# A two-block network on one core: memory laid out transposed, a split per-layer product, and an inverse that is transposed

## The chip, the cores and the metric

The kernel runs on one core of one Trainium2 chip. Its time is that of one execution on the device, in microseconds (us); three runs give a median. A profile of one further execution shows every instruction of each engine: TensorE (PE) with its weight loads (PEld), VectorE (DVE), ScalarE (ACT), GpSimd (POOL), and SyncE (SP), which issues nearly all DMAs.

## The reference

All of it is float32. There are 256 tokens of width 1024, which pass through two blocks of two layers each; everything is needed to float32 precision.

```python
def first_block(x, p, ...):                    # layers 0 and 1
    h = x
    for layer in range(2):
        hn = rmsnorm(h, gains[0])
        mix = mixer_ab(hn, ...) if layer == 0 else mixer_c(hn, ...)
        h = h + rmsnorm(mix, gains[1])
        ff = square(relu(rmsnorm(h, gains[2]) @ w_up)) @ w_down      # 1024 x 4096 x 1024
        h = h + rmsnorm(ff, gains[3])
        gate = sigmoid(h @ w_ple_gate)                               # 1024 x 1024
        h = h + gate * (p[layer] @ w_ple)                            # p: 256 x 256, w_ple: 256 x 1024
    return h

def gated_delta_rule(...):                     # in mixer_ab: 4 heads, chunks of 64 tokens
    lmat = where(strict, (kb @ k.T) * decay, 0)
    uw = triangular_solve(lmat + eye, rhs)     # the inverse of a unit lower triangular matrix
    ...

def second_block(x, mem, ...):                 # two layers more
    for l in range(2):
        xn = rms_norm(x, attn_norm[l])
        # five groups of heads on xn @ w_in[l]; the fifth attends to the memory:
        mem_kv = rms_norm(mem, mem_norm[l]) @ mem_w_kv[l]            # mem: 256 x 1024, 1024 x 512
        x = x + concat(o_a, o_b, o_c, o_d, o_e) @ w_o[l]
        xn = rms_norm(x, ffn_norm[l])
        x = x + (silu(conv(xn @ ffn_w_gate)) * (xn @ ffn_w_up)) @ ffn_w_down
```

## The kernel before

**Products.** A float32 value is split in two parts of a type for which PE needs one pass (fp32r): `hi`, the rounded copy, and `lo`, the rest. A product is then three matmuls, hi x hi, lo x hi and hi x lo. Plain float32 operands go through PE in two passes. `block` (L770) fetches 1 MB of weights into one of two tiles `raw` (512 KB and less for some), and splits it in four parts: a copy to one of four tiles `hi` (ACT, or DVE where that is free) and a subtraction to one of four tiles `lo` (DVE). `whole` (L783) loads a block straight into a `hi` tile and leaves it in plain float32. `aTh` and `aTl` hold the two parts of the transposed activations. `stream` runs a list of blocks through three matmuls for each product; `nmm` issues those of one slice, `tmm` those whose result comes out transposed.

**Stages, with the stretch of the profiled execution.** The first mixer with the delta rule (10 to 202 us; its weights are w0g, w0t, w0n and w0o), the first feed-forward (211 to 394, wu and wd), the gate of layer 0 (398 to 422, wg), the second mixer (424 to 512, w1n and w1o), the second feed-forward (522 to 704) and its gate (707 to 731), then the second block: mixers of layer 0 (731 to 891, wk, wi, wm, wo), its gated feed-forward (897 to 1088, fg, fu, fd), the mixers of layer 1 (1088 to 1234) and its feed-forward (to 1425).

**The order.** The code doesn't issue instructions as it runs: a recorder collects every operation (so nearly all rows of the profile carry its line, L610), and a list scheduler then sets the order of the whole program on every engine, operation by operation, from a table of prices (`price`), of delays between engines (`LAG`), and of the tiles that each pool has. Coroutines (`loom`) yield where work of other parts may be put between. `per_layer_input` is thus only a place in the recorded program: its matmuls are used as filler wherever the planner sees PE free and their operands ready. The borders between stages, where the residual, a norm and the transposes of the next input run, have little other work.

**What the change touches.** The inverse in the delta rule (a loop over six levels, for two pairs of heads, each with 4 matrices of 128x128 side by side): a level has a product `mb` with X, a copy, and two products `yb` and `xb` that give the next Y and the next X, which is Y's transpose. `per_layer_input` (called for layer 0 ahead of the first feed-forward and for layer 1 ahead of the second mixer) computes p @ w_ple in plain float32. `memory_T` and `memory` load the memory (four DMAs for each of the two layers of the second block), multiply it with a gain that is spread over all partitions (a DMA of 512 KB), find its root mean square, transpose it on PE, and run wk's product.

Of the kernel before, what the change touches and what calls it, by code (L numbers as in the profile page):

```python
# [50 lines left out]
for _l in range(2):  # L51
    for _n in ("mla_q", "mla_k", "fox_q", "fox_k", "moba_q", "moba_k", "diff_q", "diff_k", "mem_q", "mem_k"):
        _put(COLS, f"{_n}{_l}", 1)
    _put(COLS, f"fconv{_l}", 22 * 4)
NCOLS = sum(w for _, w in COLS.values())

# [81 lines left out]
def layout(x):  # L138
    f32 = np.float32
    A = {}  # L140
    A["x"] = x["x"].reshape(2, P, D)
    A["memx"] = x["mem_2"].reshape(2, P, D)
    pp = x["p"].reshape(2, 256, 2, P)
    A["pT"] = pp.transpose(0, 3, 2, 1).reshape(2, P, 512)
# [58 lines left out]
    for l in range(2):  # L203
        setc(f"mla_q{l}", np.concatenate([one[:32], x["mla_q_norm_2"][l][32:]]))
        setc(f"mla_k{l}", np.concatenate([one[:32], x["mla_k_norm_2"][l][32:]]))
        for s in ("q", "k"):
            setc(f"fox_{s}{l}", np.concatenate([x[f"fox_{s}_norm_2"][l], one[:1]]))
            m = np.concatenate([one[:16], x[f"moba_{s}_norm_2"][l][16:]])
            setc(f"moba_{s}{l}", np.tile(m, 2))
            d = np.concatenate([one[:8], x[f"diff_{s}_norm_2"][l][8:]])  # L210
            setc(f"diff_{s}{l}", np.tile(d, 4))
            setc(f"mem_{s}{l}", np.tile(x[f"mem_{s}_norm_2"][l], 2))
        cw = np.concatenate([x["ffn_conv_w_2"][l], x["ffn_conv_b_2"][l][None]], 0)
        setc(f"fconv{l}", cw.reshape(4, 22, P).transpose(2, 1, 0).reshape(P, 88))
# [40 lines left out]
class Recorder:  # L255
# [9 lines left out]
           "pool": {"pe": 200, "act": 90, "dve": 69, "pool": 97, "sp": 1220},  # L265
           "sp": dict.fromkeys(("pe", "act", "dve", "pool", "sp"), 910)}

# [121 lines left out]
    def price(self, op, out, ins):  # L389
# [18 lines left out]
        if op.eng == "pool":  # L408
# [4 lines left out]
            return 235 + 5 * n if op.call == "tensor_tensor" else 260 + 4 * n + 190 * per_row  # L413
        return 50 + P * n * (2 if out.dtype == BF16 else 4) / 366.0

# [242 lines left out]
def program(ctx, tc, A, out, dbg=None):  # L658
# [33 lines left out]
    def f(ap):  # L692
        return ap.bitcast(F32)
# [42 lines left out]
    aTl = cpool.tile([P, 8, 256], F32R, name="aTl")  # L736
    cpool.tile([P, 16], F32, name="behind")

# [31 lines left out]
    def block(name, i, k, w):  # L770
# [10 lines left out]
        return fold(hi[:, :n], k), fold(lo[:, :n], k)  # L781

    def whole(name, i, k, w):  # L783

        t = rec.new("hi", NHL, hlp.tile([P, 2048], F32R, tag="hi", name=nm("hi")))
        n = k * w
        sp.dma_start(out=f(t[:, :n]), in_=A[name][i])
        return fold(f(t[:, :n]), k)

# [302 lines left out]
    def mixer_ab(end):  # L1092
# [109 lines left out]
        def delta(hp):  # L1202
# [39 lines left out]
            for lv in range(1, 7):  # L1242
# [10 lines left out]
                for i in range(4):  # L1253
                    pe.matmul(yb[:, i, :], m[:, i, :], Y[:, i, :], start=True, stop=True)
                if lv < 6:
                    xb = wk(4)
                    for i in range(4):
                        pe.matmul(xb[:, i, :], Y[:, i, :], m[:, i, :], start=True, stop=True)
                    xn = w2(4)
                    dve.tensor_tensor(xn, X, xb, op=OP.subtract)  # L1260
                    X = xn
                yn = w2(4)
                dve.tensor_tensor(yn, Y, yb, op=OP.subtract)
                Y = yn
            yield
            hs = slice(2 * hp, 2 * hp + 2)
# [227 lines left out]
    def per_layer_input(l):  # L1494

        pr, pw = w2(2), {}
        sp.dma_start(out=flat(pr), in_=A["pT"][l])
        w = whole(f"wp{l}", 0, 2, 1024)
        for t in range(2):
            pw[t] = [w2(), w2()]  # L1500
            for q in range(2):
                b = acc()
                for k in range(2):
                    pe.matmul(b, pr[:, k, ts(t)], halves(w[:, k, :])[q], start=(k == 0), stop=(k == 1))
                rec.copy(pw[t][q], b, 0.5)
        return pw
# [102 lines left out]
    def heads_T(t, x, dst, k, g):  # L1609

        b = transposes([x(i) for i in range(4)])
        for i in range(2):
            rec.copy(dst[i][:k, :, ts(t)], b[:k, 2 * i : 2 * i + 2, :], col(g)[:k])

    def memory_T(l):

        g = gain(12 + l)
        parts, r = {}, {}

        def chain(t):  # L1620
            xm, xs = [w2(), w2()], [w2(), w2()]
            for q in range(2):
                sp.dma_start(out=xm[q], in_=A["memx"][t][:, q * 512 : (q + 1) * 512])
                dve.tensor_tensor(xs[q], xm[q], halves(g)[q], op=OP.mult)
            r[t], _ = rms(xm)
            yield
            for q in range(2):
                parts[t, q] = four_T(xs[q])
                yield

        for t in range(2):
            loom.spawn(chain(t), ("memT", l, t))
        return parts, r

    def memory(l, parts, r):

        kT, v = w2(2), {}

        def prep(t, bank):
            x = w2()  # L1640
            rec.copy(x, bank, r[t])
            kn = w2(8)[:, 0:4, :]
# [8 lines left out]

        loom.join(("memT", l, 0), ("memT", l, 1))
        stream(f"wk{l}", [(0, 0, 0), (0, 1, 4)], lambda t, k: parts[t, k // 4](k % 4), 4, 1, 512, tail_lagged(2, 2), done)
        return kT, v
# [416 lines left out]

    pw = per_layer_input(1)
    mixer_c(rc, out1)
# [11 lines left out]

    ff1(1, e, pw, into2)
    mem = memory(0, *memory_T(0))
    tab, lam = rope_tables2(0)
# [3 lines left out]
    for l in range(2):  # L2092
# [30 lines left out]
        if l == 0:  # L2123
            mem = memory(1, *memory_T(1))
        ff2(l, after)
# [22 lines left out]
```

## Time and profile before

| | |
|---|---|
| median of three runs | 1430.82 us (1430.28 to 1437.37) |
| profiled execution | 1430.91 us, span 1429.1 us |
| PE, PEld busy | 1383.2 us (97%), 1208.5 us (85%) |
| DVE, ACT, POOL busy | 991.2 us (69%), 765.7 us (54%), 119.6 us (8%) |
| mean granted clock of PE | 0.993 of full speed |
| DMA | 236.33 MB, 165 GB/s, 45% of the 16 engines' span |

The span is the stretch from the first to the last instruction that the profiler saw; the time of the execution has 1.8 us around it. A row of stretches gives the width, and for each engine its busy time and in brackets its instructions; PEclk is the granted clock of TensorE as a part of the full 2.4 GHz (0.5 is the lower level, 1.2 GHz). In a row such as `ps<-hi,w 128*128 128x512`, the target stands ahead of the arrow, then the moving operand, then the stationary one; ps is PSUM, w a working tile in SBUF, cf the constants (with the identity for transposes). Two passes of a plain float32 matmul count as two instructions.

### The profile page before, as it was taken

The page shows a single profiled execution, that of the slowest core. Times are in us where ns is not written, and L with a number is a line of the kernel's source. Part 1 is how long each engine was busy: PE and PEld are TensorE (multiplying, and loading weights), DVE is VectorE, ACT ScalarE, POOL GpSimd, SP SyncE. Part 2 cuts the span into 40 slices and gives each one's busy share as a digit, 9 for nine tenths or more (in the row PEclk, how much of TensorE's full clock was granted, in tenths as well). Part 3 has the DMA queues.
Part 4 walks back from the last instruction along what each step waited for, and adds up shares of the span by engine and source line. Part 5 has one row for each costly group of instructions (what it writes and reads, how often), then busy time and mean ns, then how long its engine had stood idle before and what let it go on. Part 6 is the DMA issues. An engine that isn't in the chain of part 4 may idle for free.

```text
span 1429.1 us, 23022 instructions
## 1 busy us (share of the span) xinstructions
PE 1383.2 (97%) x8824; PEld 1208.5 (85%) x8830; DVE 991.2 (69%) x2196; ACT 765.7 (54%) x1760; POOL 119.6 (8%) x140
## 2 busy tenths in 40 slices
PE   6999999999999979999999899999999999999998
PEld 6889879898877669999887777999998777799997
DVE  5995685655677865666768786665757877566664
ACT  5534564443554844444656596554545778464443
POOL 0000120000010010000024301000001511000000
PEclk9999999999999989999999999999999999999999
DMA  8412354545525353455555433345534532345443
GB/s 335 149 60 94 129 191 150 205 180 199 210 103 213 122 189 148 177 187 225 205 172 177 151 130 118 119 177 204 210 147 160 202 140 89 119 152 202 177 179 116
DMA packets 36109, 236.33 MB, mean 165 GB/s; under 512 B 4128, under 2 KB 4384, under 8 KB 9888
## 3 DMA queue, kind: packets, MB, share of 16 engines
q1 hardware_dynamic: 36000, 234.87, 45.4%
q8 instruction: 69, 1.13, 0.3%
q14 instruction: 40, 0.33, 0.1%
HBM read 233.81 MB, written 1.05 MB: 164 GB/s over the span
## 4 chain that ended last, share of the span: by engine, by line
PE 77%; DVE 12%; DMA 4%; ACT 3%; POOL 2%; issue 1%; POOLq 0%; SPq 0%; ACTq 0%; DVEq 0%
PE ps L610 77%; DVE w L610 5%; DVE lo L610 4%; POOL s L610 2%; DVE s L610 2%; ACT w L610 2%; DMA raw<-in_wu 2%; DMA raw<-in_w0t 1%; ACT hi L610 1%; DVE h L610 1%; DMA raw<-in_wg 1%; DMA raw<-in_w1n 0%; DMA raw<-in_wd 0%; ACT L610 0%; DVE aTl L610 0%
## 5 line engine op out<-in xcount | busy, mean ns | idle before, releaser
L610 ACT ACTIVATE hi<-raw 128x512 fp32r<-128x512 f32 (+2 forms) x767 | 424.3, 622 | 381.2 <-PE ps L610 281.9
L610 DVE TENSOR_TENSOR lo<-raw,hi 128x512 fp32r<-128x512 f32 x836 | 520.9, 678 | 66.4 <-ACT hi L610 63.0
L610 PE MATMUL ps<-hi,w 128*128 128x512 f32 (+1 forms) x1272 | 385.5, 401 | 0.3 <-ACT w L610 0.3
L610 PE MATMUL ps<-aTh,hi 128*128 128x256 f32 x1256 | 321.2, 281 | 2.1 <-ACT hi L610 2.1
L610 PE MATMUL ps<-aTl,hi 128*128 128x256 f32 x1256 | 321.8, 280 | 0.2 <-DVE aTl L610 0.2
L610 PE MATMUL ps<-aTh,lo 128*128 128x256 f32 x1256 | 317.5, 281 | 0.0
L610 PEld LDWEIGHTS ps<-hi,w 128*128 128x128 f32 x1272 | 222.0, 188 | 36.7 <-issue 3.8
L610 PEld LDWEIGHTS ps<-aTh,hi 128*128 128x128 f32 x1256 | 226.0, 188 | 13.5 <-ACT hi L610 3.3
L610 PEld LDWEIGHTS ps<-aTl,hi 128*128 128x128 f32 x1256 | 226.6, 188 | 9.4 <-issue 0.9
L610 PEld LDWEIGHTS ps<-aTh,lo 128*128 128x128 f32 x1256 | 224.7, 188 | 10.4 <-issue 0.7
L610 PE MATMUL ps<-lo,w 128*128 128x512 f32 (+1 forms) x620 | 200.0, 393 | 0.0
L610 ACT ACTIVATE w<-ps 128x512 f32<-128x512 f32 (+5 forms) x259 | 125.1, 532 | 132.2 <-PE ps L610 127.1
L610 DVE CAST hi<-raw 128x512 fp32r<-128x512 f32 x69 | 29.4, 426 | 239.2 <-PE ps L610 237.4
L610 PE MATMUL ps<-hi,aTh 128*128 128x512 f32 (+2 forms) x480 | 149.5, 373 | 4.3 <-ACT w L610 3.0
L610 PE MATMUL ps<-lo,aTh 128*128 128x512 f32 (+2 forms) x480 | 147.0, 369 | 2.5 <-DVE lo L610 2.5
L610 PE MATMUL ps<-hi,aTl 128*128 128x512 f32 (+2 forms) x480 | 146.6, 368 | 0.0
L610 POOL TENSOR_TENSOR s<-s,nhalf 128x1 f32<-128x1 f32 (+6 forms) x64 | 80.7, 1269 | 584.9 <-DVE s L610 582.4
L610 PEld LDWEIGHTS ps<-lo,w 128*128 128x128 f32 x620 | 109.2, 188 | 16.6 <-issue 0.7
L610 PE MATMUL ps<-cf,w 128*128 128x128 f32 (+1 forms) x564 | 96.2, 283 | 27.1 <-DVE w L610 12.9
L610 PE MATMUL ps<-w,w 128*128 128x128 f32 (+10 forms) x992 | 116.0, 299 | 3.3 <-ACT w L610 1.8
L610 ACT ACTIVATE w<-w 128x512 fp32r<-128x512 f32 (+5 forms) x145 | 75.2, 534 | 80.3 <-DVE w L610 80.0
L610 PEld LDWEIGHTS ps<-w,w 128*128 128x128 f32 (+4 forms) x992 | 96.6, 175 | 22.1 <-ACT w L610 8.3
(101 smaller groups left out, 1171.8 us busy)
## 6 DMA issues: line engine op xcount, KB each, us to landing
raw<-in_wu SPq DMA_DIRECT2D x32, 1024.0 KB, 4.8
raw<-in_wd SPq DMA_DIRECT2D x32, 1024.0 KB, 4.9
raw<-in_fg SPq DMA_DIRECT2D x22, 1024.0 KB, 4.8
raw<-in_fu SPq DMA_DIRECT2D x22, 1024.0 KB, 4.9
raw<-in_fd SPq DMA_DIRECT2D x22, 1024.0 KB, 4.8
raw<-in_wi SPq DMA_DIRECT2D x20, 1024.0 KB, 4.8
raw<-in_w0t SPq DMA_DIRECT2D x10, 1024.0 KB, 6.6
raw<-in_wo SPq DMA_DIRECT2D x10, 1024.0 KB, 4.8
```

The lines of the kernel that those rows point to most:

```text
L610: getattr(self.engines[op.eng], call)(*args, **kwargs)
```

## The change

Five edits. (1) The host's layout also holds the memory transposed (`memT`, four pieces of 256 KB), and its gains as columns of the resident `cols`; `memory_rms` finds the root mean square once for both layers. (2) `per_layer_input` uses `block` and three split matmuls for each product; the call for layer 1 moves behind the second mixer in the recorded program. (3) In five of the six levels of the inverse, X comes from a transposition of Y and a copy. (4) The pad "behind" grows from 16 to 48 columns; with 16 more columns of `cols` and two tiles `mr` the tiles behind them move. (5) The planner's prices of a DMA: 2050 ns for 910 and 400 bytes a nanosecond for 366.

```diff
     A["memx"] = x["mem_2"].reshape(2, P, D)
+    A["memT"] = x["mem_2"].reshape(256, 4, 2, P).transpose(1, 3, 2, 0).reshape(4, P, 512)
...
+        setc(f"memg{l}", x["mem_norm_2"][l].reshape(8, P).T)
...
-           "sp": dict.fromkeys(("pe", "act", "dve", "pool", "sp"), 910)}
+           "sp": dict.fromkeys(("pe", "act", "dve", "pool", "sp"), 2050)}
...
-        return 50 + P * n * (2 if out.dtype == BF16 else 4) / 366.0
+        return 50 + P * n * (2 if out.dtype == BF16 else 4) / 400.0
...
-    cpool.tile([P, 16], F32, name="behind")
+    cpool.tile([P, 48], F32, name="behind")
...
                 for i in range(4):
                     pe.matmul(yb[:, i, :], m[:, i, :], Y[:, i, :], start=True, stop=True)
-                if lv < 6:
-                    xb = wk(4)
-                    for i in range(4):
-                        pe.matmul(xb[:, i, :], Y[:, i, :], m[:, i, :], start=True, stop=True)
-                    xn = w2(4)
-                    dve.tensor_tensor(xn, X, xb, op=OP.subtract)
-                    X = xn
                 yn = w2(4)
                 dve.tensor_tensor(yn, Y, yb, op=OP.subtract)
                 Y = yn
+                if lv < 6:
+                    yield
+                    xb = transposes([Y[:, i, :] for i in range(4)])
+                    X = w2(4)
+                    rec.copy(X, xb)
...
     def per_layer_input(l):
-        pr, pw = w2(2), {}
+        pr, ph, pl, pw = w2(2), w2(2, F32R), w2(2, F32R), {}
         sp.dma_start(out=flat(pr), in_=A["pT"][l])
-        w = whole(f"wp{l}", 0, 2, 1024)
+        split_into(ph, pl, pr)
+        hi, lo = block(f"wp{l}", 0, 2, 1024)
         for t in range(2):
-            pw[t] = [w2(), w2()]
+            banks, pw[t] = [acc(), acc()], [w2(), w2()]
+            for k in range(2):
+                nmm(banks, (ph[:, k, ts(t)], pl[:, k, ts(t)]), hi[:, k, :], lo[:, k, :], k == 0, k == 1)
             for q in range(2):
-                b = acc()
-                for k in range(2):
-                    pe.matmul(b, pr[:, k, ts(t)], halves(w[:, k, :])[q], start=(k == 0), stop=(k == 1))
-                rec.copy(pw[t][q], b, 0.5)
+                rec.copy(pw[t][q], banks[q], 0.5)
         return pw
...
+    def memory_rms():
+        for t in range(2):
+            xm = [w2(), w2()]
             for q in range(2):
                 sp.dma_start(out=xm[q], in_=A["memx"][t][:, q * 512 : (q + 1) * 512])
...
+            r = cpool.tile([P, 32], F32, name=f"mr{t}")[:, 0:1]
...
+    def memory_T(l):
+        parts = []
+        for i in range(4):
+            raw, hi, lo = w2(2), w2(2, F32R), w2(2, F32R)
+            sp.dma_start(out=flat(raw), in_=A["memT"][i])
+            for j in range(2):
+                g = col(f"memg{l}", 2 * i + j)
+                rec.copy(hi[:, j, :], raw[:, j, :], g)
+                dve.scalar_tensor_tensor(lo[:, j, :], raw[:, j, :], g, f(hi[:, j, :]), op0=OP.mult, op1=OP.subtract)
+            parts.append((hi, lo))
+        return parts
...
-    pw = per_layer_input(1)
     mixer_c(rc, out1)
...
-    ff1(1, e, pw, into2)
-    mem = memory(0, *memory_T(0))
+    ff1(1, e, per_layer_input(1), into2)
+    memory_rms()
+    mem = memory(0, memory_T(0))
```

The order of the instructions changes in nearly every part of the program. Three places on PE follow; the number behind a name tells one tile from another, and x4 stands for four instructions of one kind in a row.

The first is the end of the second mixer, behind its last output projection (ps896 and ps897, weights hi907 and lo908 of w1o). Before, the transposes of the next input follow at once (cf is the identity):

```order
L610 MATMUL ps896_988<-hi907_999,w809_901 128x512
L610 MATMUL ps897_989<-hi907_999,w809_901 128x512
L610 MATMUL ps897_989<-lo908_1000,w809_901 128x512
L610 MATMUL ps897_989<-hi907_999,w809_901 128x512
L610 MATMUL ps941_1033<-cf_76,w939_1031 128x128 x3
L610 MATMUL ps923_1015<-cf_76,w921_1013 128x128 x2
```

There are now the matmuls of the second per-layer input behind the last one of the projection (ps891); hi946 and lo947 are the parts of its weights, w943 and w944 those of p:

```order
L613 MATMUL ps891_983<-lo902_994,w803_895 128x512
L613 MATMUL ps891_983<-hi901_993,w803_895 128x512
L613 MATMUL ps952_1044<-hi946_1038,w943_1035 128x512
L613 MATMUL ps952_1044<-lo947_1039,w943_1035 128x512
L613 MATMUL ps948_1040<-hi946_1038,w943_1035 128x512
L613 MATMUL ps952_1044<-hi946_1038,w944_1036 128x512
L613 MATMUL ps948_1040<-lo947_1039,w943_1035 128x512
```

All 24 of them stand ahead of the gate and the feed-forward there, 16 of them in one piece, where before this product stood at three earlier places.

The second place is the inverse in the first mixer. Before, ps172 is a product `xb` (moving w170, the copy m; stationary w167, Y), ps171 the `yb` beside it, ps125 the `mb` of the other pair of heads; ps246 is a projection with weights w0t (hi244, lo245):

```order
L610 MATMUL ps246_338<-aTh_84,hi244_336 128x256
L610 MATMUL ps172_264<-w170_262,w167_259 128x128 x4
L610 MATMUL ps171_263<-w167_259,w170_262 128x128 x4
L610 MATMUL ps246_338<-aTl_85,hi244_336 128x256
L610 MATMUL ps246_338<-aTh_84,lo245_337 128x256
L610 MATMUL ps246_338<-aTh_84,hi244_336 128x256
L610 MATMUL ps125_217<-w122_214,w124_216 128x128 x4
L610 MATMUL ps176_268<-w173_265,w175_267 128x128 x4
```

Now ps115 holds the transposes of Y (w114), ps118 the next `mb` (moving w116, the copied X); ps166 are the transposes of the other pair; ps251 belongs to w0t and ps280 to w0n:

```order
L613 MATMUL ps115_207<-cf_76,w114_206 128x128 x4
L613 MATMUL ps251_343<-aTh_84,hi249_341 128x256
L613 MATMUL ps251_343<-aTl_85,hi249_341 128x256
L613 MATMUL ps251_343<-aTh_84,lo250_342 128x256
L613 MATMUL ps251_343<-aTh_84,hi249_341 128x256
L613 MATMUL ps251_343<-aTl_85,hi249_341 128x256
L613 MATMUL ps280_372<-hi278_370,aTh_84 128x512
L613 MATMUL ps251_343<-aTh_84,lo250_342 128x256
L613 MATMUL ps280_372<-lo279_371,aTh_84 128x512
L613 MATMUL ps280_372<-hi278_370,aTl_85 128x512
L613 MATMUL ps118_210<-w116_208,w117_209 128x128
L613 MATMUL ps166_258<-cf_76,w165_257 128x128 x4
```

Between a pair's transposes and its next product there are matmuls of w0t and w0n; X's product is gone.

The third place is the end of the second block's first mixers, behind the last matmul of its output projection (ps1667 before, ps1668 now). Before, transposes of the memory follow (w1704 and w1719, then w1705 and w1720), and two matmuls of wk between the transposes of the next input (ps1699); hi1734 and lo1735 are wk's parts:

```order
L610 MATMUL ps1667_1759<-hi1680_1772,w1451_1543 128x512
L610 MATMUL ps1711_1803<-cf_76,w1704_1796 128x128
L610 MATMUL ps1726_1818<-cf_76,w1719_1811 128x128
L610 MATMUL ps1711_1803<-cf_76,w1704_1796 128x128
L610 MATMUL ps1726_1818<-cf_76,w1719_1811 128x128
```

Now wk's matmuls stand there (hi1716 and lo1717 are its parts, w1703 and w1704 those of the memory):

```order
L613 MATMUL ps1668_1762<-hi1681_1775,w1452_1546 128x512
L613 MATMUL ps1718_1812<-hi1716_1810,w1703_1797 128x512
L613 MATMUL ps1729_1823<-hi1716_1810,w1703_1797 128x512
L613 MATMUL ps1718_1812<-lo1717_1811,w1703_1797 128x512
L613 MATMUL ps1729_1823<-lo1717_1811,w1703_1797 128x512
L613 MATMUL ps1718_1812<-hi1716_1810,w1704_1798 128x512
```

The 16 transposes of the memory are replaced by 20 matmuls of wk in a row, and the transposes of the next input come behind them.

## Rows read from the trace of the kernel before

**Rows 1.** The page: span, and busy time of each engine.
```profile
span 1429.1 us, 23022 instructions
PE 1383.2 (97%) x8824; PEld 1208.5 (85%) x8830; DVE 991.2 (69%) x2196; ACT 765.7 (54%) x1760; POOL 119.6 (8%) x140
```

**Rows 2.** The page: the chain that ended last, by engine.
```profile
PE 77%; DVE 12%; DMA 4%; ACT 3%; POOL 2%; issue 1%; POOLq 0%; SPq 0%; ACTq 0%; DVEq 0%
```

**Rows 3.** Waits of PE: us in total, times, longest.
```profile
PE ps L610 <- DVE w L610: 14.3, 7, 7.6
```

**Rows 4.** Stretches: width, busy (instructions) by engine, PEclk, DMA share, GB/s.
```profile
64.00:82.00 18.00, 14.29 (x111) 12.97 (x109) 18.00 (x44) 9.29 (x23) 0.00 (x0) 0.99 0.33 117
82.00:202.00 120.00, 119.84 (x771) 107.89 (x772) 85.65 (x263) 52.83 (x126) 7.85 (x11) 0.99 0.32 115
202.00:212.00 10.00, 8.02 (x33) 4.32 (x32) 8.08 (x14) 8.63 (x24) 3.76 (x6) 1.00 0.47 157
393.00:400.00 7.00, 5.80 (x28) 3.42 (x27) 6.54 (x12) 5.42 (x14) 2.37 (x3) 1.00 0.59 195
422.00:437.00 15.00, 14.60 (x68) 10.83 (x67) 9.32 (x17) 6.83 (x15) 4.81 (x5) 1.00 0.45 175
511.00:524.00 13.00, 4.88 (x22) 3.95 (x21) 11.79 (x21) 8.33 (x23) 5.76 (x7) 0.66 0.52 187
519.40:523.00 3.60, 3.06 (x13) 2.57 (x14) 3.60 (x7) 2.31 (x6) 1.39 (x2) 0.50 0.46 146
703.00:708.00 5.00, 4.36 (x32) 3.80 (x31) 4.62 (x10) 4.39 (x12) 1.92 (x2) 1.00 0.28 116
776.00:796.00 20.00, 14.86 (x53) 11.23 (x52) 16.83 (x53) 12.52 (x25) 7.18 (x7) 0.83 0.63 209
890.00:898.00 8.00, 6.94 (x49) 5.53 (x48) 7.15 (x13) 8.00 (x20) 1.88 (x3) 1.00 0.29 120
```

**Rows 5.** PE's timeline in the first mixer: start, length, instructions, idle before.
```profile
80.31 1.16 PE L610 MATMUL ps<-w,w 128*128 128x128 f32 x8 [1.41 <-DVE w L610]
...
103.03 11.78 PE L610 MATMUL ps<-w,w 128*128 128x128 f32 x104
```

**Rows 6.** PE's timeline at two borders: transposes, and the gate's first matmul.
```profile
703.86 1.47 PE L610 MATMUL ps<-cf,w 128*128 128x128 f32 x12
...
890.57 1.91 PE L610 MATMUL ps<-cf,w 128*128 128x128 f32 x16
892.81 0.50 PE L610 MATMUL ps<-hi,w 128*128 128x512 f32 x1 [0.33 <-ACT w L610]
...
897.16 0.28 PE L610 MATMUL ps<-aTh,hi 128*128 128x256 f32 x1
```

**Rows 7.** The page's groups: count, busy us, mean ns, idle before.
```profile
L610 ACT ACTIVATE w<-ps 128x512 f32<-128x512 f32 (+5 forms) x259 | 125.1, 532 | 132.2 <-PE ps L610 127.1
```

**Rows 8.** PE's timeline at the end of the first mixer.
```profile
202.13 4.68 PE L610 MATMUL ps<-hi,w 128*128 128x512 f32 x11
```

**Rows 9.** PE's timeline in the second mixer's output projection.
```profile
505.31 1.98 PE L610 MATMUL ps<-hi,w 128*128 128x512 f32 x8
```

**Rows 10.** PE's timeline behind that projection.
```profile
519.40 1.94 PE L610 MATMUL ps<-cf,w 128*128 128x128 f32 x8 [7.59 <-DVE w L610]
```

**Rows 11.** The loads of wp: ns min/median/max, first and last start.
```profile
L610 SPq DMA_DIRECT2D hi<-in_wp x2: 327/328/328, 20.2 to 35.7; - x2
```

**Rows 12.** The page's DMA issues: count, KB each, us to landing.
```profile
raw<-in_wu SPq DMA_DIRECT2D x32, 1024.0 KB, 4.8
```

**Rows 13.** Groups of ACT: table loads.
```profile
L610 ACT ACT_TABLE_LOAD x12 | 15.4, 1283 | 6.1 <-DVE w L610 5.2 <-PEq L2138 0.7
```

**Rows 14.** Groups of PE, shapes apart.
```profile
L610 PE MATMUL ps<-hi,w 128*128 128x512 f32 x1256 | 382.2, 402 | 0.3 <-ACT w L610 0.3
L610 PE MATMUL ps<-hi,aTh 128*128 128x512 f32 x320 | 112.1, 413 | 3.4 <-ACT w L610 3.0 <-ACT hi L610 0.4
```

**Rows 15.** A stretch, instructions with tile cf alone: PE, PEld, DVE, clock.
```profile
837.00:843.00 6.00, 4.10 (x34) 3.66 (x33) 0.00 (x0) 1.00 0.01 3
```

More of the change, by code (lines that the diff above doesn't have):

```diff
@@ L54 @@
     _put(COLS, f"fconv{_l}", 22 * 4)
+    _put(COLS, f"memg{_l}", 8)
 NCOLS = sum(w for _, w in COLS.values())
@@ L781, in block @@
         return fold(hi[:, :n], k), fold(lo[:, :n], k)
[L783 to L788, printed above, removed]
     def split_into(hi, lo, src):
@@ L1613, in heads_T, with memory @@
             rec.copy(dst[i][:k, :, ts(t)], b[:k, 2 * i : 2 * i + 2, :], col(g)[:k])
[L1615 to L1621, printed above, removed]
+    mem_r = []
+    def memory_rms():
+        for t in range(2):
+            xm = [w2(), w2()]
             for q in range(2):
                 sp.dma_start(out=xm[q], in_=A["memx"][t][:, q * 512 : (q + 1) * 512])
[L1624 to L1635, printed above, removed]
+            r = cpool.tile([P, 32], F32, name=f"mr{t}")[:, 0:1]
+            a, b = meansq(xm, D)
+            x = small(1)
+            rec.scalar(x, a, b, EPS, op0=OP.add, op1=OP.add)
+            pool.tensor_tensor(r, x, nhalf[:, :1], op=OP.pow)
+            mem_r.append(r)
+    def memory_T(l):
[9 more added lines that the diff above has]
+        return parts
+    def memory(l, parts):
         kT, v = w2(2), {}
@@ L1640, in prep @@
             x = w2()
-            rec.copy(x, bank, r[t])
+            rec.copy(x, bank, mem_r[t])
             kn = w2(8)[:, 0:4, :]
@@ L1650, in done @@
             loom.spawn(prep(t, banks[0]), ("mem", l, t))
-        loom.join(("memT", l, 0), ("memT", l, 1))
-        stream(f"wk{l}", [(0, 0, 0), (0, 1, 4)], lambda t, k: parts[t, k // 4](k % 4), 4, 1, 512, tail_lagged(2, 2), done)
+        stream(f"wk{l}", [(0, 0, 0), (0, 1, 4)], lambda t, k: tuple(x[:, k % 2, ts(t)] for x in parts[k // 2]), 4, 1, 512,
+               tail_lagged(2, 2), done)
         return kT, v
@@ L2123, in program @@
         if l == 0:
-            mem = memory(1, *memory_T(1))
+            mem = memory(1, memory_T(1))
         ff2(l, after)
```

## The prediction

> **What bounds the kernel now.** The page first: TensorE (PE) is busy 97% of a 1429.1 us span [rows 1], and the chain that ended last runs on PE for 77% and on VectorE (DVE) for 12% [rows 2]. So two things count: how much work PE has, and where it stands idle. The waits of PE put 14.3 us down to DVE, the longest of them 7.6 [rows 3]. The table of stretches [rows 4] says where idle time lies: width minus PE busy. The stretch 82:202 has 119.84 us of 120 busy: there, work taken from PE is time. The stretches 202:212, 393:400, 511:524, 703:708 and 890:898 are borders between layers, with 2.0, 1.2, 8.1, 0.6 and 1.1 us idle: a residual, a norm and transposes run on DVE and ScalarE (ACT), and whatever independent matmuls exist are put there as filler. Work taken out of a border comes back as idle time. Every term below turns on which of the two kinds of place it stands in.
>
> **The inverse (delta).** Five of six levels, for two pairs of heads, lose one product of 4 matmuls 128x128 in fp32 and get 4 transposes: 40 matmuls against 40 transposes. A matmul is two passes; 104 passes took 11.78 us [rows 5], 0.113 each, 0.226 a matmul. 12 transposes took 1.47 us and 16 took 1.91 [rows 6], so 0.11 each. PE loses 40 x (0.226 - 0.11) = 4.6 us, all in the first mixer. The new chain is longer: X waits for Y's subtraction, 4 transposes (0.44) and a copy (0.53 [rows 7]), where its product stood beside Y's before; with the 0.33 that PE waited for such a copy elsewhere [rows 6] that is 1.3 a level. The order at the second place shows matmuls of other weights between the steps: that is the cover. Bounds: -4.6, and +13 with all ten levels in the open (the third rival). I take -4.6, as 82:202 is full of PE work.
>
> **The per-layer input.** Before, 16 matmuls of 512 columns in fp32, two passes each. One row holds ten of these passes behind one split matmul: 4.68 us [rows 8]; less 0.23 for that one and some 0.15 by which the last one's end is late (an estimate), 0.43 a pass, 13.8 us for 32. After, 48 split matmuls at some 0.227 (8 in 1.98 us, a late end included [rows 9]): 10.9 us. The difference of 2.9 is not what decides, the places are. Layer 0: 12 of its 16 passes stand in 202:212, whose length the chain sets; its 24 new matmuls (5.4 us) go there again. The 4 passes outside are gained: -1.7. Layer 1: its 16 passes (6.9 us) stand in 393:400 (6), 422:437 (4) and 462:474 (6). In the order at the first place its 24 new ones (5.4 us) stand right behind the last output projection, where PE idled 7.6 us before its next transposes [rows 10]: they cost nothing there. In 393:400 the 2.6 us come back as idle; of the other 4.3, taken from stretches with little idle time (0.4 of 15 us in 422:437), I give half back: -2.1. Bounds 0 and -4.3.
>
> In 511:524 the granted clock is 0.66 and in 519.4:523 it is 0.50 [rows 4]: after the 7.6 us idle PE goes on at 1.2 GHz, and 8 transposes take 1.94 us [rows 10] where 12 took 1.47 elsewhere. With 5.4 us of the hole filled I expect 2.4 GHz. The work of 519.4:523, 3.06 us, would be half as long, -1.5, and what follows it a little shorter: -2, bounds 0 and -3.
>
> **Memory.** 32 transposes of memory go. 16 stand from 703.86 on (12 in the row shown) and 16 at 890.57 [rows 6], both in borders. At 703 they go for nothing (idle comes back): 0, bound -1.7. At 890 the order at the third place shows wk1's matmuls where they stood, 20 in a row, and the order has 7 more up to just behind the gate's first; before there were 5. These 22 stood, by the order, inside the gated feed-forward's stretch, which PE fills: 22 x 0.227 = 5.0 leave it. The border was 6.6 us from its first transpose to the gate's first matmul (897.16 - 890.57); its PE work is now 27 x 0.227 + 16 x 0.11 = 7.9, longer by some 1.5. I take -3.5, bounds -1.7 (the transposes alone) and -5. Loads are neutral: 8 + 4 DMAs of 256 KB for 8 of 256 and two gains of 512. DVE and ACT do the split from SBUF instead of PSUM, in stretches where neither sets the pace.
>
> **Buffers for weights.** wp0 and wp1 were loaded at 20.2 and 35.7 us [rows 11] straight into two of the four hi tiles, and stayed there until their last passes, in 202:212 and 462:474. So only two weight blocks could be split ahead in 64:82, where PE idles 3.7 us [rows 4] in waits of the inverse, such as 1.41 for DVE [rows 5]. After, they pass through quickly, and the order has other weights between the steps there. -3; bounds +1 (the same waits elsewhere) and -5.
>
> **Prices of DMAs in the planner.** A block of 1 MB was planned at 50 + 2865 + 910 ns, 3.8 us, and is now planned at 4.7, where the trace has 4.8 to landing [rows 12]. This moves almost every row of the order. It can help at waits for weights, as in 776:796, with 5.1 us idle and a clock of 0.83 [rows 4]; it may as well make a new one of that kind. I take 0, bounds -7.6 (5.1, and 0.17 x 14.86 = 2.5 for the clock) and +5 (another such wait). **Two more table loads** on ACT in the first mixer, 1.28 us each [rows 13]: ACT is busy 52.83 of 120 us there, so 0; uncovered +2.6. **Addresses.** The columns grow by 128 bytes, "behind" by 128, two mr tiles by 128 each: hi, lo and w move by 512, aTh and aTl by 128. Matmuls with aTh as the stationary tile show 413 ns, those with w 402 [rows 14]. If all of these 11 ns were the address, 960 such matmuls (320 in each of three products) could move by 10.6 us either way; I take 0, as nothing says which way.
>
> **Sum.** -4.6 - 1.7 - 2.1 - 2 + 0 - 3.5 - 3 = -16.9. The profiled execution took 1430.91 us (span 1429.1 and 1.8 around it), the median of the runs is 1430.82, so the base is the same: **1414 us**. With the memory, the buffers and the second per-layer input at either of their nearer bounds, this case alone gives 1405 to 1424.
>
> **Rivals.**
> First, *the fillers were free*: what is taken from PE outside the inverse comes back as idle time. For it: 18 of the 32 passes and all 32 transposes stand in borders. Against it: the hole of 7.6 us takes 5.4 us of work, and the order shows that. It leaves -4.6 - 1.7: 1425.
> Second, *the new prices also end the waits behind weights*: 776:796 gives its 7.6 back. For it: the planned landing is now within 0.1 us of the traced one. Against it: raw has two tiles before and after, so that a load can't start earlier than a tile is free. 1414 - 7.6 = 1406.
> Third, slower: *the longer inverse sets the length of the first mixer*. Its price is ten levels x 1.3 = 13 in the open and 2.6 for the table loads, which then lie in front of its copies on ACT; of the other gains, 12.3, half is left, as the weights that now fill the inverse's gaps are missing later. 1431 + 13 + 2.6 - 6 = 1441. It decides from the point where PE idles more than 4.6 us between the start of the inverse and the output projection. For it: the chain does get longer, and PE waits for DVE there now. Against it: 119.84 of 120 busy, and filler between the steps.
> Fourth, slower too: *the transposes let PE's clock fall*. The inverse's products and transposes are 10 x (8 x 0.226 + 4 x 0.11) = 22 us of PE; at 1.2 GHz they take 22 more, and with the other gains of 12 that is 1431 + 22 - 12 = 1441. Against it: in 837:843 transposes make up 4.10 of 6 us, and the granted clock is 1.00 [rows 15], the higher level of 2.4 GHz.
> The Trainium skill, page "TensorE: Matmul & The Clock Gate", Part 4 (PE-mode transpose), says that transposes don't count as work for the clock, so that full speed doesn't engage for them: this is what would bring the fourth rival about. By that rule the clock of 837:843 should be the lower one; the trace doesn't agree.
> That the change doesn't do what it says is excluded by the order: the 40 products are gone from PE's rows.
>
> **How the numbers follow.** Within 0.5% (7 us) is about what a measurement of this kernel can't tell from no change: 1423.7 and 1438 are the borders. Chances: the forecast 0.58, fillers free 0.18, waits behind weights gone too 0.12, chain 0.10, clock 0.02. Faster: nearly all of the forecast (0.55), all of the second rival and a third of the first (0.06): 0.73. Slower: 0.09 (three quarters of the last two). Same: the rest, 0.18. The range reaches from some way below the second rival, 1400, to the slow side of the first, 1432; what is left out is most of the third and fourth rivals and a tail below.
>
> **What would show each step.** Right: PE without idle time from the start of the inverse to the output projection, and that stretch shorter by 4 us or more; the 24 per-layer matmuls behind the last output projection of the second layer, with the clock at 1.00 behind them; idle at the gate of the first layer grown to about 3 us; 27 matmuls of wk1 at the border after the second block's first mixers; the idle of 64:82 mostly gone. Wrong: PE idle over 5 us inside the first mixer, the lower clock in the inverse, new waits of PE for lo or hi in stretches that are full now, or a pitch of the split matmuls off 0.227, which would be the addresses.

## The result, and the profile after

The changed kernel takes 1400.32 us (median of four runs, 1399.66 to 1401.15); the kernel before, run beside it, 1433.35 (1430.28 to 1437.37). The ratio is 0.9768 with a 95% interval of [0.9738, 0.9799], some 33 us (29 to 37) by it. In three later series of 14 to 21 runs the kernel before had medians of 1431.0 to 1431.2, by which the gain is nearer 31. The forecast was 17 us; the time lies 0.3 us inside the lower edge of the range.

The page of the kernel after, span and busy times:

```profile
span 1399.4 us, 22914 instructions
PE 1362.3 (97%) x8767; PEld 1200.1 (86%) x8774; DVE 979.3 (70%) x2182; ACT 786.1 (56%) x1800; POOL 119.5 (9%) x132
...
PE 83%; DVE 7%; ACT 4%; POOL 2%; DMA 2%; issue 1%; SPq 0%; ACTq 0%; DVEq 0%
```

Against [rows 1, 2], PE's work fell by 20.9 us and the rest of the span by 8.8 (45.9 to 37.1). DVE's share of the chain fell from 12% to 7%. The stretches that answer to six of those in [rows 4], in the same order of places (width, busy and instructions by engine, granted clock, DMA share, GB/s):

```profile
64.00:82.00 18.00, 17.76 (x150) 17.24 (x149) 18.00 (x43) 12.71 (x31) 0.00 (x0) 1.00 0.47 176
82.00:189.00 107.00, 107.00 (x680) 95.55 (x679) 79.12 (x244) 60.14 (x137) 9.10 (x13) 1.00 0.39 138
377.00:384.00 7.00, 3.65 (x16) 3.18 (x15) 6.18 (x11) 5.12 (x13) 1.55 (x2) 0.69 0.41 150
494.00:507.00 13.00, 12.46 (x81) 10.94 (x80) 13.00 (x23) 10.93 (x27) 3.38 (x5) 1.00 0.38 121
751.00:771.00 20.00, 16.29 (x73) 12.85 (x72) 14.92 (x63) 10.89 (x23) 10.01 (x7) 0.83 0.56 204
863.00:872.00 9.00, 9.00 (x51) 7.66 (x50) 8.12 (x15) 7.55 (x18) 1.89 (x3) 1.00 0.27 108
```

The first mixer has no idle time from 82 to 189 us, and 64:82 has 0.2 us in place of 3.7. The gate of the first layer (377:384) has 3.4 us of idle time where it had 1.2, and some 3 were expected; its clock fell to 0.69 from 1.00, which the prediction did not price. The border behind the second mixer (494:507) has 0.5 us idle in place of 8.1, and its clock is 1.00 for 0.66. The place that waited for weights at 776 has 3.7 us idle (here 751:771) in place of 5.1, with the same clock. The border at 863 is full and lasts 7.3 us to the first matmul of the next feed-forward, against 6.6.

Cut at the last matmul of each weight, the 29.9 us by which PE's last matmul came earlier divide up so: the first mixer 12.4, the border behind it 2.0, the first feed-forward 2.1, its gate -2.0, the second mixer 2.9, its border 4.5, feed-forward and gate 1.1, the second block's first mixers 3.7, border -0.9, feed-forward 3.4, mixers -2.7, border 1.0, and the last feed-forward 2.3, which has the same 1336 instructions of PE before and after.

### The profile page after: what moved, and what is told of

The parts are those of the page before. It is cut to its first block, busy times and chain, and to the rows that moved or that the text cites. A ratio compares the mean times of both kernels' runs of the same rounds, so it can differ in the third digit from the quotient of the medians.

```text
span 1399.4 us, 22914 instructions
## 1 busy us (share of the span) xinstructions
PE 1362.3 (97%) x8767; PEld 1200.1 (86%) x8774; DVE 979.3 (70%) x2182; ACT 786.1 (56%) x1800; POOL 119.5 (9%) x132
## 4 chain that ended last, share of the span: by engine, by line
PE 83%; DVE 7%; ACT 4%; POOL 2%; DMA 2%; issue 1%; SPq 0%; ACTq 0%; DVEq 0%
PE ps L613 83%; DVE w L613 4%; ACT w L613 2%; POOL s L613 2%; DMA raw<-in_w0t 2%; DVE lo L613 1%; DVE s L613 1%; ACT hi L613 1%; DVE h L613 1%; DMA raw<-in_wi 0%; ACT L613 0%; ACT aTh L613 0%; DVE aTl L613 0%; SPq L613 0%; DVE hi L613 0%
## 5 line engine op out<-in xcount | busy, mean ns | idle before, releaser
L613 ACT ACTIVATE hi<-raw 128x512 fp32r<-128x512 f32 (+1 forms) x793 | 436.5, 619 | 296.7 <-PE ps L613 241.0
L613 DVE TENSOR_TENSOR lo<-raw,hi 128x512 fp32r<-128x512 f32 (+2 forms) x844 | 524.5, 677 | 55.9 <-ACT hi L613 52.4
L613 PE MATMUL ps<-hi,w 128*128 128x512 f32 (+1 forms) x1272 | 378.9, 395 | 0.0
L613 PE MATMUL ps<-aTl,hi 128*128 128x256 f32 x1256 | 317.2, 280 | 0.0
L613 PEld LDWEIGHTS ps<-aTh,lo 128*128 128x128 f32 x1256 | 223.6, 189 | 10.1 <-DVE lo L613 0.9
L613 PE MATMUL ps<-lo,w 128*128 128x512 f32 (+1 forms) x636 | 207.5, 394 | 0.0
L613 ACT ACTIVATE w<-ps 128x512 f32<-128x512 f32 (+3 forms) x261 | 126.1, 525 | 124.5 <-PE ps L613 116.3
L613 DVE CAST hi<-raw 128x512 fp32r<-128x512 f32 x51 | 21.8, 426 | 174.2 <-PE ps L613 174.2
L613 PEld LDWEIGHTS ps<-lo,w 128*128 128x128 f32 x636 | 113.6, 188 | 17.3 <-issue 0.7
L613 PE MATMUL ps<-w,w 128*128 128x128 f32 (+9 forms) x912 | 108.3, 299 | 0.4 <-ACT w L613 0.2
L613 PEld LDWEIGHTS ps<-w,w 128*128 128x128 f32 (+4 forms) x912 | 88.9, 172 | 18.4 <-issue 7.0
```

The costliest lines, as they stand in the source:

```text
L613: getattr(self.engines[op.eng], call)(*args, **kwargs)
```

## The experiments

Theory A was the prediction's: every part gives what its work and its holes are worth. Theory B put the surplus on the planner's prices, theory C on addresses, theory D on the inverse. All ratios are to the kernel before, run beside each.

| run | median us | ratio | 95% interval |
|---|---|---|---|
| the inverse alone | 1425.09 | 0.9959 | 0.9944 to 0.9975 |
| the per-layer input alone | 1420.59 | 0.9936 | 0.9917 to 0.9955 |
| the memory alone, new addresses | 1427.69 | 0.9972 | 0.9956 to 0.9987 |
| both prices alone | 1416.80 | 0.9912 | 0.9894 to 0.9931 |
| delay alone | 1416.41 | 0.9882 | 0.9861 to 0.9904 |
| delay zero | 1431.29 | 0.9999 | 0.9985 to 1.0013 |
| spare columns | 1422.99 | 0.9926 | 0.9903 to 0.9948 |
| same order, moved | 1425.60 | 0.9962 | 0.9947 to 0.9976 |
| per-layer call not moved | 1425.51 | 0.9951 | 0.9935 to 0.9968 |
| all but the prices | 1415.11 | 0.9876 | 0.9851 to 0.9902 |
| all but the pad | 1403.69 | 0.9813 | 0.9797 to 0.9829 |
| the whole, delay 2600 | 1400.74 | 0.9790 | 0.9776 to 0.9805 |

**Each part alone.** The first four took one part of the diff each, the third with the new addresses too. The inverse alone (the diff's edit in the loop over levels):

> The kernel before with the transposed inverse alone. Theory A (work and holes, as predicted): PE loses 40 x (0.226 - 0.11) = 4.6 us in the first mixer and its idle time there stays near 5.3 us: about 4 to 6 us faster in all. Theory B (the planner's prices carry most of the surplus): also 4 to 6. Theory C (addresses carry the surplus): also 4 to 6, as nothing moves in memory. Theory D (the inverse itself gives the 12.4 us by which the first mixer of the changed kernel is shorter): 10 us or more faster.

Measured: 5.9 us faster by the ratio (3.6 to 8.0). Theory A's 4 to 6 holds, theory D doesn't. PE's work in the first mixer and its idle time both fell: this is the stretch from PE's first instruction to the end of that mixer, first in the kernel before (5.3 us idle), then in this run (4.1).

```profile
10.60:202.50 191.90, 186.58 (x1264) 168.37 (x1266) 148.64 (x399) 95.32 (x215) 7.85 (x11) 0.99 0.42 150
10.60:196.50 185.90, 181.84 (x1225) 162.96 (x1226) 142.93 (x390) 100.19 (x225) 7.85 (x11) 1.00 0.43 155
```

The clock is 1.00 there, with 40 transposes more. The per-layer input alone, with its second call moved:

> The kernel before with the split per-layer product alone, its second call moved behind the second mixer. Theory A: the hole behind the second mixer is filled and two hi tiles come free early: -1.7 - 2.1 - 2 - 3, some 6 to 9 us faster. Theories B and C: no more than the passes that leave full stretches, 2 to 6 us. If the hole filled is worth its whole 5.4 us and the clock behind it, 9 to 11.

Measured: 9.2 us faster (6.4 to 11.9); the prediction's four terms for it sum to 8.8. Two stretches of its profile show the two holes filled:

```profile
504.90:510.70 5.80, 5.80 (x28) 4.52 (x26) 5.80 (x11) 5.80 (x16) 1.96 (x3) 1.00 0.53 171
64.00:82.00 18.00, 17.94 (x148) 17.32 (x148) 17.93 (x44) 11.72 (x27) 0.00 (x0) 1.00 0.51 177
```

The border behind the second mixer lasts 5.8 us, all of it busy at the full clock, where before it lasted 10.1. And 64:82 lost its idle time with the inverse untouched. That the two hi tiles that come free did this, as the prediction had it, isn't shown: 64:82 is also full with the prices alone and with a delay of zero (both below), where wp0 and wp1 are loaded into hi tiles at 13.6 and 32.9 us, and at 32.5 and 40.8, and still used at 200 and 460 us. These are the two, in that order:

```profile
64.00:82.00 18.00, 18.00 (x155) 17.66 (x154) 17.77 (x42) 6.70 (x17) 0.00 (x0) 1.00 0.17 59
64.00:82.00 18.00, 17.97 (x150) 17.69 (x151) 18.00 (x44) 12.64 (x30) 0.00 (x0) 1.00 0.42 170
```

Another order is enough to fill it.

> The kernel before with the transposed memory, and with the pad of 48 columns, so that all addresses are those of the changed kernel. Theory A: 3.5 us faster from the 32 transposes and wk1's matmuls at the border. Theory C (addresses): 10 us or more, and the pitch of matmuls with aTh moving (128x256) at 114 ns instead of 118. Theory B: 3 to 4.

Measured: 4.0 us faster (1.9 to 6.3), but it has the new addresses, which alone are worth 5.4 (below). So nothing is left for the memory itself, within some 3 us. The border got 0.9 us longer and the gated feed-forward behind it 5.0 shorter, as many as forecast, but not for the reason given. This is the feed-forward in the kernel before and in this one:

```profile
897.10:1087.70 190.60, 190.60 (x1354) 178.41 (x1354) 124.01 (x223) 93.37 (x179) 0.00 (x0) 1.00 0.50 179
```

```profile
896.20:1081.80 185.60, 185.60 (x1341) 173.68 (x1340) 121.30 (x219) 92.70 (x178) 0.00 (x0) 1.00 0.51 184
```

PE has 13 instructions less there, not 22: some 3 us. About 1.8 us come from the places of the tiles (see the addresses below). The rest of wk1's matmuls that now stand in the border came out of the next mixers, and those got 6.2 us longer. This is that stretch in the kernel before and in this one:

```profile
1087.70:1180.20 92.50, 91.10 (x470) 75.38 (x470) 74.66 (x213) 66.99 (x176) 33.00 (x26) 1.00 0.43 156
```

```profile
1081.80:1180.50 98.70, 92.62 (x457) 75.43 (x455) 72.97 (x212) 64.33 (x170) 32.98 (x24) 0.97 0.40 146
```

There are fewer matmuls, and 6.1 us idle for 1.4, at a clock of 0.97 for 1.00. Its border at 700 us also has PE idle for 3.7 us where 16 transposes of the memory stood.

> The kernel before with the planner's new prices of a DMA alone (2050 ns and 400 bytes a nanosecond). Theory A: between 7 faster and 5 slower, near 0. Theory B: 10 us or more faster, with the idle time at 776:796 gone. Theory C: near 0.

Measured: 12.6 us faster (9.9 to 15.2). This is theory B's result, and outside the bounds of the prediction's term.

**What the prices do.** The edits were 910 to 2050 alone, and 910 to 0 alone:

```diff
-           "sp": dict.fromkeys(("pe", "act", "dve", "pool", "sp"), 910)}
+           "sp": dict.fromkeys(("pe", "act", "dve", "pool", "sp"), 0)}
```

> The kernel before with the delay of a DMA priced at 2050 ns, the rate left at 366 bytes a nanosecond: 1 MB is planned at 5.0 us. Theory M (the gain comes from copies on ACT that were planned ahead of a transfer's landing, and held up what was queued behind them): about as fast as with both prices, 11 to 16 us faster than before, and ACT's waits for raw at some 50 us in place of some 77. Theory N (a reordered program lands anywhere within 10 us of another): no relation to that figure.

> The kernel before with the delay of a DMA priced at 0 ns in place of 910: 1 MB is planned at 2.9 us, 1.9 under the traced 4.8. Theory M: 5 to 15 us slower than before, with more waits of ACT for raw than its 77 us. Theory N: either side of before with the same chance.

The delay alone gives all of it, 16.9 us (13.8 to 19.9). The other direction missed: a plan of 2.9 us is as fast as one of 3.8, not slower. So there is no slope; these few orders would fit a step between plans of 3.8 and 4.7 us, with the traced landing at 4.8. Theory M's sign missed as well. ACT's waits for raw add up to 76.9 us before, 50.1 with both prices, but 65.5 with the delay alone, which is no slower, and 82.4 with the delay at zero. The same order as before with its tiles moved (below) has 89.2, and is faster. Nor do the lines of the place that the second rival named show what theory M says. First ACT's timeline in the kernel before (start, length, idle time before and what ended it), then PE's:

```profile
783.70 2.19 ACT L610 ACTIVATE hi<-raw 128x512 fp32r<-128x512 f32 x4 [5.42 <-DMA raw<-in_wi]
787.06 0.60 ACT L610 ACTIVATE w<-ps 128x512 f32<-128x512 f32 x1 [1.17 <-PE ps L610]
...
788.65 2.18 ACT L610 ACTIVATE hi<-raw 128x512 fp32r<-128x512 f32 x4
...
791.60 1.21 ACT L610 ACTIVATE w<-ps,cols 128x256 f32<-128x256 f32 x3
```

```profile
780.09 0.73 PE L610 MATMUL ps<-lo,aTh 128*128 128x512 f32 x2 [1.97 <-DVE lo L610]
...
791.77 0.79 PE L610 MATMUL ps<-hi,aTh 128*128 128x512 f32 x1 [3.01 <-ACT w L610]
```

ACT stood 5.4 us, to 783.70, before a copy whose block had not landed. But PE waited 2.0 us for a split before that, to 780.09, and then worked without a longer gap than 0.2 us to 788.8, past the end of ACT's stand; behind its copy ACT was idle again, for PE. PE's wait of 3.0 us, to 791.77, came when ACT copied another block (788.65, 2.18 us) ahead of the pieces of a norm; the granted clock of 776:796 was 0.83 [rows 4]. So there is a bad order around the weights, and that the late landing made it isn't shown. With both new prices the longest wait of ACT for a block there is this one:

```profile
774.74 2.19 ACT L610 ACTIVATE hi<-raw 128x512 fp32r<-128x512 f32 x4 [0.82 <-DMA raw<-in_wi]
```

In the changed kernel, which has the new prices too, such waits are no shorter than before (us in total, times, longest; before, then after):

```profile
ACT hi L610 <- DMA raw<-in_wi: 10.8, 6, 5.4
ACT hi L613 <- DMA raw<-in_wi: 14.3, 8, 5.8
```

With both prices alone the stretch of these mixers, up to the last of wi's matmuls, went from 108.1 to 102.4 us. Over the whole program the span less PE's busy time went from 45.9 to 36.1 us, and PE's busy time itself from 1383.2 to 1377.4. With the delay at zero, idle time was 41.2 and PE busy 1387.9: there the waits moved, and the sum stayed. That the new prices gave a better order each time they were tried (both, the delay alone, and in the whole, below) is shown. That it is so because they are truer isn't: with the delay at zero the mixers' stretch got as short (102.3), and the border behind the second mixer shorter still, 5.3 us against 7.1 with the new prices and 10.1 before:

```profile
515.50:520.80 5.30, 1.11 (x5) 0.72 (x4) 5.30 (x11) 5.30 (x14) 0.93 (x1) 0.75 0.53 151
```

That order lost as much elsewhere. Theory N, that another order lands some us off whatever the reason, isn't excluded for a part of the gain; the run with spare columns (below) speaks for it.

> The changed kernel with the old prices of a DMA (910 ns, 366 bytes a nanosecond). If the parts add up, the three others give 6.1 + 10.6 + 3.5 = 20 us: 20 us faster than before, 10 to 11 slower than the changed kernel. If the prices only mend what the other parts mend too (the waits of the inverse and the border behind the second mixer), 25 or more faster than before. If the other parts need the prices to be worth anything, under 15.

Measured: 17.7 us faster (14.0 to 21.3); the three other parts alone sum to 5.9 + 9.2 + 4.0 = 19.1. So the parts add up, and the prices still give the 15 us between 1415.11 and 1400.32 when the rest is there.

> The changed kernel with the delay of a DMA at 2600 ns: 1 MB is planned at 5.3 us, above nearly every traced landing. Theory M (the plan has to be no earlier than the landing): as fast as the changed kernel or up to 5 us faster, with ACT's waits for raw under its 49.5 us. Theory N (the gain of a price is the luck of an order): anywhere within 10 us, with no relation to ACT's waits.

Measured: 1400.74, the same as the changed kernel. This plan, later than the landing, is worth no more. It doesn't beat the changed kernel, and no run here does.

**The call that moves.** The split product with the call left in its old place:

> The kernel before with the split per-layer product, its second call left ahead of the second mixer: the order has 6 of its 24 matmuls behind the last output projection there, 18 before it. Theory A (the hole filled is 4 of the 9 to 10 us of the per-layer part): 3 to 5 us slower than with the call moved, 5 to 7 faster than before, the border behind the second mixer as long as before less 1.4. If the buffers that come free are all of it: as fast as with the call moved.

Measured: 7.0 us faster by the ratio (4.6 to 9.3), against 9.2 with the call moved; by medians 4.9 apart, with runs that overlap. Its border was expected at 8.7 us and lasts 4.7 us, with 2.7 idle: this order has less of DVE's chain in it (10 instructions of DVE, 16 before), so the length of the hole was not fixed. What the move does show is the clock. These are the border before, then with the call left the border, the feed-forward behind it, and ten microseconds from 1.4 us behind the border on:

```profile
511.80:521.90 10.10, 1.98 (x10) 1.49 (x9) 8.88 (x16) 7.15 (x20) 3.94 (x4) 0.67 0.58 208
```

```profile
505.70:510.40 4.70, 2.01 (x11) 1.22 (x9) 4.70 (x10) 4.70 (x12) 0.93 (x1) 0.97 0.47 134
510.40:695.40 185.00, 184.76 (x1174) 167.03 (x1175) 117.01 (x198) 86.19 (x168) 2.56 (x5) 0.98 0.53 197
```

```profile
511.80:521.80 10.00, 10.00 (x66) 10.00 (x66) 7.58 (x13) 3.22 (x8) 2.37 (x4) 0.74 0.39 139
```

With the call moved, the feed-forward behind the border of 5.8 us:

```profile
510.70:692.50 181.80, 181.73 (x1175) 164.10 (x1175) 115.03 (x195) 85.66 (x166) 3.00 (x5) 1.00 0.53 198
```

With the call left, PE is idle for 2.7 us in the border and then works at a clock of 0.74 over ten microseconds that have no gap; with as much work, that feed-forward is 3.2 us longer. The slow time behind the gap costs about as much as the gap.

**Addresses.** First with spare columns in place of the new ones:

> The kernel before with spare columns and tiles, so that every tile has the address it has in the changed kernel, and not one instruction moved. Theory C (addresses): the 2 us by which the last feed-forward is shorter in the changed kernel and in the one with the transposed memory alone come from here: 2 to 8 us faster, matmuls with aTh moving at a pitch of 114 ns for 118. Prediction: 0, and that the pitch differs from run to run.

It was 10.6 us faster by the ratio, but my premise failed: the wider `cols` is a longer DMA in the plan, and the order differs over the first 900 matmuls, in the first mixer. (With the 5.4 us of the next run taken off, some 5 us are left, though the two intervals just touch. If they are real, another order of the first mixer is worth that much, with no price made truer.) The next run moves the same tiles without touching a DMA:

```diff
-    cpool.tile([P, 16], F32, name="before")
+    cpool.tile([P, 48], F32, name="before")
...
-    cpool.tile([P, 16], F32, name="behind")
+    cpool.tile([P, 112], F32, name="behind")
```

> The kernel before with its two pads wider, by 128 and by 384 bytes: all operand tiles of PE stand at the addresses of the changed kernel, and the order is the one of before, instruction by instruction (the run with spare columns had an order of its own in the first mixer). Theory C (addresses): 3 to 8 us faster, in the stretches of the feed-forwards above all, 2 in the last one. Prediction (addresses do nothing): within 2 us of before, and the last feed-forward as long as before.

Measured: 5.4 us faster (3.4 to 7.6), with every instruction in the same order. Theory C holds; the prediction's 0 doesn't. The gated feed-forward of the second block's first layer went from 190.6 us (its row stands with the memory, above) to 188.8, with the same 1354 instructions:

```profile
890.90:1079.70 188.80, 188.80 (x1354) 176.61 (x1354) 123.95 (x223) 93.08 (x179) 0.00 (x0) 1.00 0.50 181
```

The last feed-forward, 1336 instructions of PE in each row, in the kernel before, moved, in the run with the prices alone (old addresses; on PE the same order here as the changed kernel), in the changed kernel, and in the changed kernel with the old pad:

```profile
1237.60:1425.40 187.80, 187.65 (x1336) 175.44 (x1336) 116.18 (x210) 82.01 (x156) 0.00 (x0) 1.00 0.44 159
```

```profile
1229.40:1416.20 186.80, 186.76 (x1336) 174.97 (x1336) 116.33 (x210) 81.83 (x155) 0.00 (x0) 0.99 0.44 160
```

```profile
1222.20:1409.80 187.60, 187.41 (x1336) 175.40 (x1336) 113.47 (x203) 86.46 (x164) 0.91 (x2) 1.00 0.44 159
```

```profile
1210.00:1395.50 185.50, 185.31 (x1336) 173.16 (x1336) 113.73 (x203) 86.75 (x164) 0.91 (x2) 1.00 0.44 161
```

```profile
1209.30:1396.90 187.60, 187.43 (x1336) 175.30 (x1336) 113.67 (x203) 86.82 (x164) 0.90 (x2) 1.00 0.44 159
```

The last one answers the other question, put to the changed kernel:

> The changed kernel with the pad back at 16 columns: hi, lo, raw and w stand 128 bytes lower, aTh and aTl where they are, and no instruction moves. Theory C: if the step of 128 bytes decides, 3 to 10 us slower than the changed kernel, with the excess spread over all stretches of weight matmuls. Prediction: the same within 2 us.

Measured: 1403.69 (1402.58 to 1405.98), 3.4 us above the changed kernel's median, whose highest run is 1401.15; the two were not run in one series, and the ratios' intervals just overlap. The traces agree with it: in the same order PE is busy 5.8 us longer (1368.1 for 1362.3), and the last feed-forward takes 2.1 us more, while idle time elsewhere fell by 4.4 us. A step of 128 bytes of the tiles behind aTl is enough, then.

The length of a row doesn't show the change (0.28 us for a matmul of 256 columns in either), the distance between starts does. Over all matmuls of 256 columns with aTh or aTl moving, its mean is 117.2 ns in the kernel before and 115.9 in the one moved, 115.9 in the changed kernel and 117.3 with the old pad. (Distances of 100 to 140 ns between two starts in the traces; longer ones are waits or lower clock.) Not every matmul changed: in either kernel there are distances near 118 and near 112, and the share under 115 went from 14% to 44%. All traces fall in two groups: 117.0 to 117.4 ns in the eight with the old places or the old pad, 115.5 to 116.0 in the six with the new ones, whatever else changed. At 1.3 ns the 3768 such matmuls make some 5 us.

## Why the prediction was right, and where its sizes were off

**The inverse** (forecast -4.6, measured -5.9, 3.6 to 8.0): right. PE's work there fell and the longer chain stayed covered: 82:189 has no idle time, and the third rival with its 13 us did not come. Nor did the fourth: the stretch 80:115 of the changed kernel, which holds most of the inverse, has this clock:

```profile
80.00:115.00 35.00, 35.00 (x271) 33.36 (x270) 27.91 (x112) 23.09 (x42) 0.00 (x0) 1.00 0.33 121
```

The 40 transposes (some 4.4 us by the prediction's 0.11 each) leave the granted clock at 1.00, as [rows 15] had suggested. The Trainium skill (page "TensorE: Matmul & The Clock Gate", Part 4, PE-mode transpose) says that full speed doesn't engage for such transposes. With so few among other matmuls this stretch is a weak test of that; the denser one of [rows 15], 4.10 of 6 us, disagrees.

**The per-layer input, the clock behind it and the buffers** (-1.7 - 2.1 - 2 - 3 = -8.8, measured -9.2, 6.4 to 11.9): right in sum, in part by luck. Idle time came back at the gate of layer 0 (3.4 us), the hole of [rows 10] is gone, and 64:82 is full. But the prediction put the new work into a hole whose length the chain of DVE sets, and gave 2 us for the clock; the border became 4.3 us shorter, and was no fixed quantity, as the run with the call left showed. And the 3 us were to come from two hi tiles, while 64:82 is as full in orders in which those stay taken.

**The memory** (-3.5; alone nothing, within 3 us, once the addresses are taken off): the step at the border did not come as forecast. The prediction read that 22 matmuls of wk1 leave the gated feed-forward, 5.0 us; PE has 13 instructions less there in the run with the memory alone, and 10 in the whole change. In the whole change that feed-forward gave 3.4 us and the border took 0.9, with some 1.8 of the former due to addresses (the stretch went from 190.6 to 188.8 us when the tiles moved in the same order). The next mixers took more back than was left: 6.2 us in the run with the memory alone, 2.7 in the whole. In the changed kernel:

```profile
871.20:1058.30 187.10, 187.10 (x1344) 175.33 (x1343) 118.31 (x213) 93.37 (x181) 0.00 (x0) 1.00 0.51 183
```

**The prices** (0, with bounds of -7.6 and +5; measured -12.6, 9.9 to 15.2): this is the step that was mis-sized, and its bound too. The prediction read one place (776:796) and made it the bound; the price acted at many. The first mixer, the first feed-forward, the border behind the second mixer and the second block's first mixers got 4, 2, 3 and 6 us shorter in the run with the prices alone. The second rival had named the prices, with 7.6 us and a chance of 0.12, but not what happened: its place still has 3.7 us idle at a clock of 0.83 in the changed kernel (751:771), where the prices give 15 us. Which waits they end, and whether they do so by being truer, stays open.

**The addresses** (0, with 10.6 us either way; measured -5.4, 3.4 to 7.6): the value lies inside the bounds, the choice of 0 was wrong. The reason given, that nothing says which way, was true; the bound was read off row lengths [rows 14], which are not what changed.

So the whole: the terms worked out from rows gave -16.9, and all parts but the prices measured -17.7, of which 5.4 are addresses that had been put at 0. Without them the worked-out terms came to about -12. So that 16.9 and 17.7 agree is luck. The direction was right, and so were the inverse and most of the places; the surplus comes from a price list, above all, that the prediction had treated as noise.

## What to carry to other kernels

When a planner orders the work, a changed price is a change to every wait in the program: bound it by all waits that such an order can make, not by one of them, and try it alone. Comparing a price with its traced duration found a better one here, though a price that was further off cost nothing. When a stretch fills, see whether it also fills in runs that lack the supposed cause. When the pitch (the distance between starts) of a long run of equal matmuls differs between kernels, move the operand tiles by 128 bytes with the order held fixed before looking for another cause; and when tiles are moved for such a test, see that no planned size changes with them.

## What the runs showed of the hardware that was not expected

Moving tiles in SBUF against each other by 128 or 384 bytes, with the same order, changed the mean pitch of split matmuls of 256 columns between 117.2 and 115.9 ns, as the share with the shorter of two values (near 112 and 118) changed. The distance from aTh to the first hi tile that the program fills was 61632 bytes in the kernel before and 61888 with the old pad (both slow), and 62016 in the changed kernel and in the one moved (both faster). The first two leave 192 over a multiple of 256 bytes, the last 64. Why the pitch depends on it, and whether raw and w matter, which moved along with hi and lo, was not tried and stays open.

With 2.7 us of idle time in a border of 4.7, the mean granted clock was 0.74 in the ten microseconds from 1.4 us behind it on, in which PE worked without a gap; behind the same border full of work (5.8 us) the feed-forward had a clock of 1.00, and was 3.2 us shorter.
